# Two transformer blocks on one core: the values' largest magnitude by a matrix product in two steps, and one projection moved ahead of the attention heads

## The chip, the cores and the metric

The kernel runs on one core of a Trainium2 chip. The core has four compute engines with a queue each, which work through their instructions strictly in order: TensorE (PE in the rows; its weight loads stand apart as PEld), VectorE (DVE), ScalarE (ACT) and GpSimd (POOL). SyncE (SP) does nothing here but issue transfers. Engines wait for one another through semaphores. The metric is the device time of one execution in microseconds.

## What is computed

Two blocks follow one another on 512 tokens of width 1024. The first has two kinds of attention and a mixture of experts; the second has a recurrence over time and a latent attention (called MLA below). Cut to what matters here:

```python
def first_block(x, ...):
    h = rms_norm(x, norm_mix_g)
    (f_q, f_k, f_v, f_f, n_q, k_c, v_c, k_s, v_s, k_w, v_w, n_g, g_a, g_b) = split_cols(h @ w_in)
    out_a = from_heads(fox_attention(qa, ka, va, log_f)) @ w_fox_up        # 8 heads of 64, causal
    out_b = from_heads(nsa_attention(qb, kc, vc, ks_, vs_, kw_, vw_, gates)) @ w_nsa_up
    x = x + (sigmoid(g_a) * out_a + sigmoid(g_b) * out_b) @ w_out
    return x + hierarchical_moe(rms_norm(x, norm_ffn_g), ...)              # 16 experts

def second_block(x, ...):
    y_a = rwkv7_branch(...)                                                # recurrence
    y_b = mla_branch(c_q, c_kv, k_pe, z_b, ...)                            # 8 heads of 64, causal
    return x + rmsnorm((g_a * y_a + g_b * y_b) @ w_o, g_post)

# in each attention:  p = softmax(q k^T ...);  out = p @ v
```

## The kernel before, in words

**Two halves.** Products are made nearly exact by splitting an operand x into a coarse part and the rest, x = xh + xl. A projection takes three products per 128 rows of weights (`mm3`: lines 118 to 120), and attention weights and values are split into two 16-bit halves. Sixteen bits have a narrow range, so `Attention.values` first scales a value tensor by 1024 over its largest magnitude. It is called four times: for the 512 value columns of the fox heads (`zv`), for two value groups of 128 columns of the NSA heads (a slice of `kv` and one of `kw`), and for the 512 columns of MLA (`v`).

**The largest magnitude.** VectorE reduces the tensor to one number per partition (`vmx`, line 395). The 128 numbers are written to device memory (line 398) and read back with each partition receiving all of them (`vrow`, line 400). VectorE reduces that row (`vma`, line 402), makes the factor `vsc` and its inverse (lines 403 to 408), ScalarE writes the coarse half (line 414) and VectorE the rest (line 415).

**Heads and fill.** `Attention.run` walks over heads; a head has three units (query tiles 0 and 1, tile 2, tile 3). In turn u it issues the scores of unit u, one preparation step of the next head, the transposes of unit u-1 and the products with the values of unit u-2. The softmax between them is done on VectorE (`s`, `m`) and ScalarE (`p`). Between these pieces `Fill.pull(rate)` issues steps of a list of other work, mostly projections: a projection of 256 columns has 32 products of three matmuls, booked at 0.32 each (3 n / 2400), and a pull of `rate` issues steps until the booked sum is reached. A step without a product has a booking too: each of the six steps that start the NSA heads (`N.start`: gates, norms, values) is booked at 1.0 and puts nothing on TensorE but VectorE and GpSimd work.

**Order.** TensorE's order is exactly that in which the code issues. The other engines' order is set by the scheduler of the build, which the code only suggests. In the first block the fill list is: projections q, k, v of the fox heads, then `kw`, `nq`, the NSA start, gates and output projections. `fill.until("v")` drains it up to the fox values before the heads begin; the rate is 2.0 up to unit 22 and 1.62 after. In MLA the rate is 1.06, and what is left of its list is pulled by the recurrence's preparation.

**Banks.** Accumulators are tiles in eight banks of PSUM. The tag `mm` (projections) has two banks, taken in turn; `x` (preparation of queries and keys) has one. A bank is free again when an engine has read its tile out.

## Time and profile before

| | us |
|---|---|
| median of 3 runs | 1434.35 |
| lowest, highest | 1432.84, 1443.26 |
| the profiled execution | 1437.92 |
| its span, first to last instruction | 1436.0 |
| TensorE busy | 1285.7 (90%) |
| VectorE busy | 951.4 (66%) |
| ScalarE busy | 753.9 (53%) |

The profiled execution is 3.57 us above the median. Busy shares are means over stages with different limits. The fox heads stand at 145 to 300 us of the span, the NSA heads up to 456, the experts at 500 to 880, MLA at 915 to 1045, the recurrence after that. In rows with a time at the front, the first number is the start in us and the second the duration in us; brackets give the idle time of the engine just before and what ended it.

### The profile page before, as it was taken

The numbers are of one execution on the slowest core, as the hardware profiler recorded it, in microseconds if no ns is written. First come the engines' busy times: TensorE is split into PE (matmuls) and PEld (weight loads), VectorE is DVE, ScalarE is ACT, GpSimd is POOL, SyncE is SP. The second block draws the span as 40 slices with busy tenths as digits, with TensorE's granted clock in tenths as the row PEclk, the third lists the DMA queues.
The fourth block names the chain that finished last, engine by engine and source line by source line (L and its number), as shares of the span: only waits on it lengthen the run. The fifth ranks groups of instructions, "written<-read, shape, count | busy, mean of one in ns | idle before, by whom it ended". The sixth has DMA issues, their size and how long they took to land.

```text
span 1436.0 us, 24621 instructions
## 1 busy us (share of the span) xinstructions
PE 1285.7 (90%) x9232; PEld 1090.5 (76%) x9232; DVE 951.4 (66%) x1907; ACT 753.9 (53%) x1291; POOL 427.3 (30%) x349
## 2 busy tenths in 40 slices
PE   7989777997989896899999997879988998799997
PEld 6889677987889775577777776868976767788875
DVE  5565557556565637799999997646657858525645
ACT  5544445665444322688888874645556664224431
POOL 1333324332332111235555522201123335213211
PEclk9999888999999998899999998989999999799999
DMA  6432222222133388999999986521152234233543
GB/s 195 119 106 76 63 54 61 86 64 66 60 96 115 98 285 328 320 356 364 355 345 359 343 292 209 148 83 48 46 165 74 83 123 123 87 100 115 169 135 118
DMA packets 162445, 230.94 MB, mean 161 GB/s; under 512 B 22426, under 2 KB 99021, under 8 KB 162320
## 3 DMA queue, kind: packets, MB, share of 16 engines
q1 hardware_dynamic: 150912, 205.44, 43.7%
q0 software_dynamic: 6224, 18.62, 4.6%
q10 hardware_dynamic: 5184, 5.25, 1.1%
q8 instruction: 74, 1.21, 0.3%
q14 instruction: 51, 0.42, 0.1%
HBM read 200.89 MB, written 30.36 MB: 161 GB/s over the span
## 4 chain that ended last, share of the span: by engine, by line
PE 37%; DVE 9%; DMA 5%; issue 5%; ACT 4%; POOL 1%; POOLq 0%; DVEq 0%; ACTq 0%; SPq 0%
PE mm L118 8%; PE mm L120 8%; PE mm L119 8%; DMA x2d<-y,slt 2%; PE s L120 2%; PE s L118 2%; PE s L119 2%; DMA raw<-in_w_in 2%; PE s L457 1%; DVE itmp L1766 1%; DVE Ti L1768 1%; DMA raw<-in_w_o 1%; PE pt L484 1%; DMA vmmx<-vmx 1%; POOL wl L112 1%
## 5 line engine op out<-in xcount | busy, mean ns | idle before, releaser
L112 POOL TENSOR_TENSOR wl<-raw,wh 128x512 fp32r<-128x512 f32 x119 | 163.7, 1381 | 462.9 <-ACT wh L109 424.2
L92 DVE TENSOR_TENSOR wl<-rawe,wh 128x1024 fp32r<-128x1024 f32 x192 | 224.8, 1218 | 23.9 <-ACT wh L90 22.9
L109 ACT ACTIVATE wh<-raw 128x512 fp32r<-128x512 f32 x214 | 131.6, 627 | 130.2 <-PE mm L120 57.6
L118 PE MATMUL mm<-wh,hh 128*128 128x256 f32 (+1 forms) x616 | 186.7, 303 | 11.1 <-ACT hh L90 3.5
L90 ACT ACTIVATE wh<-rawe 128x1024 fp32r<-128x1024 f32 x192 | 190.6, 1052 | 2.0 <-PE mm L120 1.8
L119 PE MATMUL mm<-wl,hh 128*128 128x256 f32 (+1 forms) x616 | 179.7, 292 | 0.3 <-DVE wl L112 0.3
L120 PE MATMUL mm<-wh,hl 128*128 128x256 f32 (+1 forms) x616 | 179.8, 292 | 0.1
L118 PEld LDWEIGHTS mm<-wh,hh 128*128 128x128 f32 (+1 forms) x616 | 122.8, 199 | 14.3 <-ACT hh L90 3.9
L1262 POOL DMA_INDIRECT xe<-td,slf x16 | 97.9, 6118 | 116.8 <-issue 73.4
L119 PEld LDWEIGHTS mm<-wl,hh 128*128 128x128 f32 (+1 forms) x616 | 122.6, 199 | 2.0 <-DVE wl L112 0.5
L120 PEld LDWEIGHTS mm<-wh,hl 128*128 128x128 f32 (+1 forms) x616 | 122.0, 198 | 0.9 <-DVE hl L92 0.4
L118 PE MATMUL mm<-wh,uh 128*128 128x256 f32 (+1 forms) x352 | 110.4, 314 | 12.9 <-DVE sg L2202 9.3
L112 DVE TENSOR_TENSOR wl<-raw,wh 128x512 fp32r<-128x512 f32 x95 | 79.4, 840 | 58.8 <-ACT wh L109 58.4
L475 ACT ACTIVATE p<-s,m 128x128 f32<-128x128 f32 (+3 forms) x128 | 67.3, 525 | 83.3 <-DVE m L471 62.6
L118 PE MATMUL mm<-wh,xh 128*96 128x512 f32 x256 | 103.8, 405 | 1.3 <-ACT xh L90 1.3
L119 PE MATMUL mm<-wl,uh 128*128 128x256 f32 (+1 forms) x352 | 104.7, 298 | 0.0
L120 PE MATMUL mm<-wh,ul 128*128 128x256 f32 (+1 forms) x352 | 104.5, 297 | 0.0
L120 PE MATMUL mm<-wh,xl 128*96 128x512 f32 x256 | 102.0, 398 | 0.4 <-DVE xl L92 0.4
L119 PE MATMUL mm<-wl,xh 128*96 128x512 f32 x256 | 101.2, 395 | 0.0
L488 DVE SCALAR_TENSOR_TENSOR pl<-pt,ph 128x384 f16<-128x384 f32 (+1 forms) x96 | 57.6, 600 | 39.1 <-ACT ph L487 38.5
L118 PEld LDWEIGHTS mm<-wh,uh 128*128 128x128 f32 x352 | 70.6, 200 | 15.6 <-DVE sg L2202 9.5
L119 PEld LDWEIGHTS mm<-wl,uh 128*128 128x128 f32 x352 | 70.7, 201 | 0.8
(717 smaller groups left out, 3390.0 us busy)
## 6 DMA issues: line engine op xcount, KB each, us to landing
raw<-in_w_in SPq DMA_DIRECT2D x71, 512.0 KB, 3.9
rawe<-in_w_gate SPq DMA_DIRECT2D x64, 512.0 KB, 10.7
rawe<-in_w_down SPq DMA_DIRECT2D x63, 512.0 KB, 11.5
rawe<-in_w_up SPq DMA_DIRECT2D x62, 512.0 KB, 12.1
gd<-sg SPq DMA_DIRECT2D x32, 128.0 KB, 1.9
g<-gd SPq DMA_DIRECT2D x16, 256.0 KB, 3.9
md<-sg ACTq DMA_DIRECT2D x32, 128.0 KB, 2.0
mix<-md SPq DMA_DIRECT2D x16, 256.0 KB, 3.8
```

What stands on the lines that cost most here:

```text
L90: nc.scalar.activation(hi, src, AF.Copy, scale=scale)
L92: nc.vector.tensor_sub(lo, src, hi.bitcast(FT))
L109: nc.scalar.activation(wh, raw[:, k:k + m], AF.Copy)
L112: e.tensor_sub(wl, raw[:, k:k + m], wh.bitcast(FT))
L118: nc.tensor.matmul(out, xh, wh, start=start, stop=False)
L119: nc.tensor.matmul(out, xh, wl, start=False, stop=False)
L120: nc.tensor.matmul(out, xl, wh, start=False, stop=stop)
L457: mm = nc.tensor.matmul(si, q[:, 128 * i:w], k[:, :w], start=a == 0, stop=a == len(passes) - 1)
L475: nc.scalar.activation(p[:, o:o + w], si, AF.Exp, bias=m, scale=-1.0)
L484: nc.tensor.transpose(pt[:, j:j + 128], p[:, j:j + 128], c.ident)
L488: nc.vector.scalar_tensor_tensor(pl[:, :w], pt[:, :w], PSC, ph[:, :w], op0=OP.mult, op1=OP.subtract)
L1262: nc.gpsimd.indirect_dma_start(out=xe, out_offset=None, in_=td, in_offset=bass.IndirectOffsetOnAxis(ap=of, axis=0))
```

## The change

`Attention.values` now returns two functions. The first does the reduction to one number per partition. The second multiplies on TensorE: the 128 numbers, repeated along 128 columns, as one operand and the identity matrix as the other, so that every partition of the result holds all 128 numbers; VectorE reduces that from PSUM. The write to memory and the read back are gone. The product takes a tile of the tag `mm`.

- Fox values: the first function runs where the whole did; the second is step 16 of the 32 products of `kw`.
- `kw` (32 products) moves ahead of the heads: `fill.until("kw")`.
- NSA: the start has eight steps in place of six, still booked at 1.0 each.
- MLA: 3.5 of fill are pulled between the two functions.
- The rate of the first block is 1.64 throughout.

```diff
--- before.py
+++ after.py
@@ -390,30 +390,34 @@
     def values(self, z, nh, pool, name):
 
 
+
         c, nc = self.c, self.c.nc
         mx = c.sm.tile([128, 1], FT, name="vmx")
-        nc.vector.tensor_reduce(mx, z, axis=AX.XY, op=OP.max, apply_absolute_value=True)
-
-        mxd = c.dram.tile([128, 1], FT, name=name + "mx")
-        nc.sync.dma_start(mxd, mx)
-        row = c.sm.tile([128, 128], FT, name="vrow", bufs=1)
-        nc.sync.dma_start(row, _ap(mxd, 0, [[0, 128], [1, 128]]))
-        ma = c.sm.tile([128, 1], FT, name="vma")
-        nc.vector.tensor_reduce(ma, row, axis=AX.X, op=OP.max)
-        nc.vector.tensor_scalar(ma, ma, 1e-30, None, op0=OP.max)
-        sc = c.sm.tile([128, 1], FT, name="vsc")
-        nc.vector.reciprocal(sc, ma)
-        nc.vector.tensor_scalar(sc, sc, PSC, None, op0=OP.mult)
-        back = c.sm.tile([128, 1], FT, name=name + "b", bufs=1)
-        nc.vector.tensor_scalar(back, ma, 1.0 / PSC, None, op0=OP.mult)
-        vh = pool.tile([128, NT, nh, 65], F16, name=name + "h", bufs=1)
-        vl = pool.tile([128, NT, nh, 65], F16, name=name + "l", bufs=1)
-        nc.gpsimd.memset(vh[:, :, :, 64:], 1.0)
-        nc.gpsimd.memset(vl[:, :, :, 64:], 0.0)
-        z = z.rearrange("p i (h d) -> p i h d", d=64)
-        nc.scalar.activation(vh[:, :, :, :64], z, AF.Copy, scale=sc)
-        nc.vector.scalar_tensor_tensor(vl[:, :, :, :64], z, sc, vh[:, :, :, :64], op0=OP.mult, op1=OP.subtract)
-        return vh, vl, back
+
+        def first():
+            nc.vector.tensor_reduce(mx, z, axis=AX.XY, op=OP.max, apply_absolute_value=True)
+
+        def second():
+
+            ps = c.bank("mm", [128, 512])[:, :128]
+            nc.tensor.matmul(ps, mx.to_broadcast([128, 128]), c.ident, start=True, stop=True)
+            ma = c.sm.tile([128, 1], FT, name="vma")
+            nc.vector.tensor_reduce(ma, ps, axis=AX.X, op=OP.max)
+            nc.vector.tensor_scalar(ma, ma, 1e-30, None, op0=OP.max)
+            sc = c.sm.tile([128, 1], FT, name="vsc")
+            nc.vector.reciprocal(sc, ma)
+            nc.vector.tensor_scalar(sc, sc, PSC, None, op0=OP.mult)
+            back = c.sm.tile([128, 1], FT, name=name + "b", bufs=1)
+            nc.vector.tensor_scalar(back, ma, 1.0 / PSC, None, op0=OP.mult)
+            vh = pool.tile([128, NT, nh, 65], F16, name=name + "h", bufs=1)
+            vl = pool.tile([128, NT, nh, 65], F16, name=name + "l", bufs=1)
+            nc.gpsimd.memset(vh[:, :, :, 64:], 1.0)
+            nc.gpsimd.memset(vl[:, :, :, 64:], 0.0)
+            zh = z.rearrange("p i (h d) -> p i h d", d=64)
+            nc.scalar.activation(vh[:, :, :, :64], zh, AF.Copy, scale=sc)
+            nc.vector.scalar_tensor_tensor(vl[:, :, :, :64], zh, sc, vh[:, :, :, :64], op0=OP.mult, op1=OP.subtract)
+            return vh, vl, back
+        return first, second
 
     def run(self, jobs, fill, rate, hooks=()):
 
@@ -647,8 +651,12 @@
 
     qs, two, fx = [], {}, {}
 
+    def largest():
+        fx["first"], fx["second"] = A.values(z["zv"], 8, at, "vf")
+        fx["first"]()
+
     def values():
-        fx["v"] = A.values(z["zv"], 8, at, "vf")
+        fx["v"] = fx["second"]()
 
     def norm(name):
         fx[name] = _head_norm(c, z["z" + name], 512, name, at)
@@ -710,8 +718,9 @@
     jobs = {}
     for name, c0 in (("q", 0), ("k", 512), ("v", 1024)):
         jobs |= {f"{name}{a}": proj("z" + name, {"q": "t0", "k": "zk", "v": "t1"}[name], c0, a) for a in (0, 256)}
-        jobs[name] = ([], [(0.5, values if name == "v" else lambda name=name: norm(name))])
+        jobs[name] = ([], [(0.5, largest if name == "v" else lambda name=name: norm(name))])
     jobs["kw"] = proj("kw", None, 2568, 0, 256)
+    jobs["kw"][1].insert(16, (0.3, values))
     jobs |= {f"nq{a}": proj("nq", "t1", 1544, a) for a in (0, 256)}
     jobs["start"] = ([], [(1.0, f) for f in N.start(A, z, gt)])
     late = []
@@ -766,9 +775,9 @@
     with tc.manual_schedule(engines={mybir.EngineType.PE}):
         N.keys(I, A, z["kv"], fill)
         N.values(I, A, z["kv"], fill)
-        fill.until("v")
+        fill.until("kw")
         comp = [f for g in range(2) for f in N.compressed(g)]
-        A.run([fox(h) for h in range(8)] + N.jobs(A, lambda: big("ob", "zk")), fill, lambda u: 2.0 if u <= 22 else 1.62,
+        A.run([fox(h) for h in range(8)] + N.jobs(A, lambda: big("ob", "zk")), fill, lambda u: 1.64,
               [(43 + 2 * n, f) for n, f in enumerate(comp)])
         fill.until(None)
 
@@ -922,13 +931,17 @@
         def norm(name, z, c0, w):
             self.r[name] = _head_norm(c, proj[z][:, :, c0:c0 + w], w, name, at)
 
-        def values(b, z, c0):
-            v = A.values(proj[z][:, :, c0:c0 + 128], 2, at, "vsw"[b::2])
+        def largest(b, z, c0):
+            self.v[b] = A.values(proj[z][:, :, c0:c0 + 128], 2, at, "vsw"[b::2])
+            self.v[b][0]()
+
+        def values(b):
+            v = self.v[b][1]()
             g = self.gt[:, :, :, b + 1]
             nc.vector.tensor_scalar(g, g, v[2], None, op0=OP.mult)
             self.v[b] = v[:2]
-        return [gates, lambda: norm("n", "nq", 0, 512), lambda: norm("s", "kv", 256, 128), lambda: values(0, "kv", 384),
-                lambda: norm("w", "kw", 0, 128), lambda: values(1, "kw", 128)]
+        return [gates, lambda: largest(0, "kv", 384), lambda: norm("n", "nq", 0, 512), lambda: largest(1, "kw", 128),
+                lambda: values(0), lambda: norm("s", "kv", 256, 128), lambda: values(1), lambda: norm("w", "kw", 0, 128)]
 
     def jobs(self, A, out):
 
@@ -2046,7 +2059,10 @@
         c.mm3(ps, ckv[:, 0, ts], ckv[:, 1, ts], wkh[:, 1].rearrange("p h n -> p (h n)"),
               wkl[:, 1].rearrange("p h n -> p (h n)"), True, True)
         nc.scalar.activation(v[:, i], ps, AF.Copy)
-    vh, vl, vb = A.values(v, 8, ml, "vm")
+    largest, values = A.values(v, 8, ml, "vm")
+    largest()
+    fill.pull(3.5)
+    vh, vl, vb = values()
 
     o = ml.tile([128, NT, 512], FT, name="o", tag="e8", bufs=3)
     z = ml.tile([128, NT, 512], FT, name="z", tag="e8", bufs=3)
```

Rows of the build's order follow. A name is the tile written, then the tiles read.

**VectorE, before the first fox head, before.** `q` and `kl` belong to the queries and keys of head 0; `vfb` and `vwb` are the inverse factors of the fox and of the second NSA values.

```order
L395 TENSOR_REDUCE vmx<-kv 128x1
L112 TENSOR_TENSOR wl<-raw,wh 128x512
L362 SCALAR_TENSOR_TENSOR q<-x,cvec,q 64x512 x2
L402 TENSOR_REDUCE vma<-vrow 128x1
L403 TENSOR_SCALAR vma<-vma 128x1
L405 RECIPROCAL vsc<-vma 128x1
L408 TENSOR_SCALAR vfb<-vma 128x1
L406 TENSOR_SCALAR vsc<-vsc 128x1
L94 SCALAR_TENSOR_TENSOR kl<-x,cvec,kh 128x512
L402 TENSOR_REDUCE vma<-vrow 128x1
L403 TENSOR_SCALAR vma<-vma 128x1
L405 RECIPROCAL vsc<-vma 128x1
```

The same place now:

```order
L405 TENSOR_REDUCE vma<-mm 128x1
L406 TENSOR_SCALAR vma<-vma 128x1
L408 RECIPROCAL vsc<-vma 128x1
L411 TENSOR_SCALAR vfb<-vma 128x1
L409 TENSOR_SCALAR vsc<-vsc 128x1
L418 SCALAR_TENSOR_TENSOR vfl<-zv,vsc,vfh 128x32x64
L112 TENSOR_TENSOR wl<-raw,wh 128x512
L398 TENSOR_REDUCE vmx<-kw 128x1
L112 TENSOR_TENSOR wl<-raw,wh 128x512
L362 SCALAR_TENSOR_TENSOR q<-x,cvec,q 64x512 x2
L94 SCALAR_TENSOR_TENSOR kl<-x,cvec,kh 128x512
```

The reduction `vma` stood between the queries and the keys of head 0; now the whole of the fox values stands ahead of both, and no NSA `vma` is near.

**VectorE at the start of the MLA heads, before.** Tile numbers are kept: `mm` tiles belong to the fill, `x` tiles to queries and keys, `sg` reads a finished fill tile out.

```order
L395 TENSOR_REDUCE vmx_12296<-v_12144 128x1
L165 SCALAR_TENSOR_TENSOR sg_12321<-sg_12321,mm_12269 128x256
L2073 TENSOR_TENSOR qf_12345<-x_12338,csq_11874 128x512
L112 TENSOR_TENSOR wl_12766<-raw_12763,wh_12765 128x512
L92 TENSOR_TENSOR ql_12386<-qf_12345,qh_12385 128x512
L2160 SCALAR_TENSOR_TENSOR sg_12359<-mm_12325,rx_y_11833,br_12267 128x256
L92 TENSOR_TENSOR kl_11971<-x_12377,kh_11970 64x512
L402 TENSOR_REDUCE vma_12302<-vrow_12300 128x1
L92 TENSOR_TENSOR kl_11973<-x_12377,kh_11972 64x512
L403 TENSOR_SCALAR vma_12302<-vma_12302 128x1
L405 RECIPROCAL vsc_12305<-vma_12302 128x1
L408 TENSOR_SCALAR vmb_12308<-vma_12302 128x1
```

The same place now:

```order
L398 TENSOR_REDUCE vmx_12290<-v_12138 128x1
L165 SCALAR_TENSOR_TENSOR sg_12295<-sg_12295,mm_12263 128x256
L112 TENSOR_TENSOR wl_12649<-raw_12646,wh_12648 128x512
L2176 SCALAR_TENSOR_TENSOR sg_12324<-mm_12299,rx_y_11827,br_12261 128x256
L405 TENSOR_REDUCE vma_12347<-mm_12345 128x1
L406 TENSOR_SCALAR vma_12347<-vma_12347 128x1
L408 RECIPROCAL vsc_12350<-vma_12347 128x1
L411 TENSOR_SCALAR vmb_12353<-vma_12347 128x1
L409 TENSOR_SCALAR vsc_12350<-vsc_12350 128x1
L418 SCALAR_TENSOR_TENSOR vml_12356<-v_12138,vsc_12350,vmh_12355 128x32x64
L2089 TENSOR_TENSOR qf_12385<-x_12378,csq_11868 128x512
L2176 SCALAR_TENSOR_TENSOR sg_12390<-mm_12338,rx_y_11827,br_12261 128x256
```

`vma` no longer stands behind `qf`, `ql` and the first `kl` but ahead of them, and `vml`, the long last step of the values, now stands ahead of the queries' `qf` and of the `sg` that reads `mm_12338` out.

**TensorE at the same place, before.** The `x` tile is the keys' product of head 0.

```order
L118 MATMUL mm_12325<-wh_12229,uh_11583 128x256
L119 MATMUL mm_12325<-wl_12230,uh_11583 128x256
L120 MATMUL mm_12325<-wh_12229,ul_11584 128x256
L118 MATMUL mm_12373<-wh_12181,uh_11583 128x256
L119 MATMUL mm_12373<-wl_12182,uh_11583 128x256
L120 MATMUL mm_12373<-wh_12181,ul_11584 128x256
L118 MATMUL x_12377<-ckv_11987,wkh_12138 128x512
L119 MATMUL x_12377<-ckv_11987,wkh_12138 128x512
L120 MATMUL x_12377<-ckv_11987,wkl_12139 128x512
```

And now, from the queries' product on:

```order
L118 MATMUL x_12378<-cq_11980,wqh_12124 128x512
L119 MATMUL x_12378<-cq_11980,wqh_12124 128x512
L120 MATMUL x_12378<-cq_11980,wql_12125 128x512
L118 MATMUL mm_12338<-wh_12223,uh_11577 128x256
L119 MATMUL mm_12338<-wl_12224,uh_11577 128x256
L120 MATMUL mm_12338<-wh_12223,ul_11578 128x256
L118 MATMUL mm_12404<-wh_12175,uh_11577 128x256
L119 MATMUL mm_12404<-wl_12176,uh_11577 128x256
L120 MATMUL mm_12404<-wh_12175,ul_11578 128x256
```

The fill tiles change here. Before, the next tile `mm_12373` follows `mm_12325` in the turn of the two banks. Now the values' product `mm_12345`, issued in the middle of `mm_12338`, has taken a turn, so that `mm_12404` gets the bank of `mm_12338` itself.

## Rows read from the trace of the kernel before

**Rows 1.** The page, part 1: span, and TensorE's line.

```profile
span 1436.0 us, 24621 instructions
PE 1285.7 (90%) x9232; PEld 1090.5 (76%) x9232; DVE 951.4 (66%) x1907; ACT 753.9 (53%) x1291; POOL 427.3 (30%) x349
```

**Rows 2.** Chain that ended last, 940 to 975 us: start, duration, what.

```profile
947.75 9.12 DMA vmmx<-vmx
956.88 3.87 DMA vrow<-vmmx
...
962.32 2.01 ACT vmh L414
964.35 2.35 DVE vml L415
```

**Rows 3.** Tile vrow, its reader's idle times: releaser, us, times.

```profile
  DMA vrow<-smx: 10.2, 1
  DMA vrow<-vmmx: 9.0, 1
  DMA vrow<-vfmx: 7.7, 1
  DMA vrow<-vwmx: 1.5, 1
```

**Rows 4.** Timeline of TensorE: waits.

```profile
162.98 0.47 PE L457 MATMUL s<-kl,q 128*128 128x128 f32 x1 [4.93 <-DVE kl L94]
...
186.08 0.47 PE L457 MATMUL s<-kl,q 128*128 128x128 f32 x1 [9.41 <-DVE kl L94]
...
251.15 0.63 PE L349 MATMUL x<-ident,two 128*128 128x128 f32 x4 [2.39 <-DVE q L362]
...
304.90 0.39 PE L118 MATMUL mm<-wh,hh 128*128 128x256 f32 x1 [1.17 <-ACT sg L155]
...
961.93 0.77 PE L118 MATMUL x<-cq,wqh 128*128 128x512 f32 x1 [6.40 <-DVE vma L403]
```

**Rows 5.** Busy time by stretch; PEclk is TensorE's granted clock.

```profile
core 0: us, PE busy (x) PEld busy (x) DVE busy (x) ACT busy (x) POOL busy (x), PEclk, DMA share, GB/s
...
163.00:168.00 5.00, 5.00 (x23) 4.89 (x23) 3.49 (x8) 3.44 (x7) 2.80 (x1) 0.50 0.04 11
...
186.10:191.80 5.70, 5.70 (x26) 5.61 (x27) 2.80 (x12) 2.53 (x5) 0.00 (x0) 0.50 0.00 0
...
221.30:234.80 13.50, 8.77 (x57) 7.40 (x57) 11.71 (x54) 5.58 (x10) 6.44 (x27) 0.55 0.22 60
...
237.00:300.00 63.00, 59.44 (x601) 56.86 (x601) 39.07 (x110) 39.77 (x77) 24.40 (x23) 1.00 0.25 75
320.00:340.00 20.00, 14.02 (x135) 11.93 (x131) 13.73 (x44) 12.30 (x24) 5.37 (x6) 1.00 0.26 74
...
961.90:973.40 11.50, 9.17 (x29) 6.91 (x29) 6.66 (x12) 6.37 (x9) 0.00 (x0) 0.50 0.24 89
```

**Rows 6.** Timeline of VectorE in MLA.

```profile
960.77 0.29 DVE L402 TENSOR_REDUCE vma<-vrow 128x1 f32<-128x128 f32 x1 [9.01 <-DMA vrow<-vmmx]
...
962.47 0.48 DVE L2160 SCALAR_TENSOR_TENSOR sg<-mm,rx_y,br 128x256 f32<-128x256 f32 x1
...
967.42 0.68 DVE L2073 TENSOR_TENSOR qf<-x,csq 128x512 f32<-128x512 f32 x1
```

**Rows 7.** Timeline of TensorE in MLA: fill and queries.

```profile
946.40 0.39 PE L118 MATMUL x<-cq,wqh 128*128 128x512 f32 x1
...
947.77 0.28 PE L118 MATMUL mm<-wh,uh 128*128 128x256 f32 x1
...
953.29 0.28 PE L118 MATMUL mm<-wh,uh 128*128 128x256 f32 x1
...
953.64 0.28 PE L118 MATMUL mm<-wh,uh 128*128 128x256 f32 x1
```

**Rows 8.** Groups by line: 128x128 32-bit products with the identity.

```profile
L349 PE MATMUL x<-ident,two 128*128 128x128 f32 x80 | 12.7, 283 | 8.4 <-DVE q L362 8.2 <-DVE pc L92 0.3
```

## The prediction

> **What bounds the kernel now.** I read the page first: TensorE is busy 90% of a span of 1436.0 us [rows 1], so time is won only where TensorE waits or runs slowly, and work that is merely moved among its steps is worth nothing. Then the tile that the change deletes. VectorE waits for the read back of the 128 numbers at all four calls, 10.2, 9.0, 7.7 and 1.5 us [rows 3], and the chain that ended last goes through the MLA call: 9.12 us for the write of 128 numbers and 3.87 for the read back [rows 2]. VectorE's queue is in order, so whatever stands behind `vma` waits with it. The timeline of TensorE shows whom that reaches: a wait of 4.93 us and one of 9.41 for the keys `kl` of fox heads, which stand behind the `vma` of the fox values and of the second NSA values, and one of 6.40 in MLA, for the `x` bank that a `kl` behind `vma` reads out [rows 4]. So three of the four round trips reach TensorE.
>
> Each wait is followed by a stretch at 1.2 GHz. The granted clock is 0.50 from 163.0 to 168.0, from 186.1 to 191.8 and from 961.9 to 973.4, with TensorE busy 5.00, 5.70 and 9.17 us in them [rows 5]. At 2.4 GHz that work takes half as long, so the waits cost another 2.5, 2.85 and 4.6 us.
>
> The Trainium skill (DMA: Bandwidth & Descriptors, section Anatomy of one DMA) puts the fixed part of a transfer at about 2.0 us, nearly all of it the confirmation of the write. By that page a pair would take 4.0 us as an estimate, not the 13.0 of rows 2; every wait of TensorE would be nearly covered already, and the change would have only its costs, below. The trace disagrees and decides.
>
> **Removed.** Waits 4.93 + 9.41 + 6.40 = 20.7, slow clock 2.5 + 2.85 + 4.6 = 10.0, together 30.7 us. The 2.3 us that TensorE also idles between 961.9 and 973.4 (9.17 busy of 11.50 [rows 5]) I leave: a softmax chain starts there in either kernel. With the eight small transfers the queue of SyncE no longer holds weight loads behind a read back; I give that nothing, since the loads it delays feed fill that TensorE reaches later.
>
> **Added: the products.** Four products with the identity at some 0.28 us [rows 8]. Those of the two NSA calls fall where TensorE waits anyway. The fox one stands after 16 of the 32 products of `kw`, about 16 x 0.35 = 5.6 us after the reduction was issued (a fill product takes 0.35: the successive starts at 953.29 and 953.64 [rows 7]), so it finds its operand. But it takes a turn of the two `mm` banks, and the third tile of `kw` must then wait until the second, just finished, is read out. The nearest row of such a wait is 1.17 us [rows 4]. Between 0.3 and 1.5 in all; I take 1.0, near that row.
>
> **Moved: `kw` ahead of the heads.** Its 32 products are 11.2 us of full TensorE work that the pulls of 2.0 in units 0 to 22 held before. The lower rate takes 23 x 0.36 = 8.3 booked, 9.1 us in real time, out of those units, and after unit 22 nothing changes to speak of (1.62 to 1.64). If TensorE is the bound in them, they shorten by the 9.1 and the move is free; if the chain of softmax, transposes and bank `x` is the bound, they don't shorten and 9.1 us of waiting appear. From 237 to 300 TensorE was busy 59.44 of 63.00 us at full clock [rows 5], so it is nearly always the bound at the old rate; the idle that is there is mostly for the queries' bank, as the 2.39 us at 251.15 [rows 4]. A tenth thinner cover will widen such waits a little: 2.0, between 0 and 9.1.
>
> **Moved: the start of the NSA heads.** Its steps are booked at 1.0 and put no fill on TensorE. Six at a rate of 2.0 were three units without fill, 221.3 to 234.8: 13.5 us, TensorE busy 8.77 at a mean clock of 0.55, VectorE busy 11.71 [rows 5]. Idle is 4.7; a clock of 0.55 means 12.1 of the 13.5 us at half speed, in which at least 7.4 were busy, which lost 3.7. So 8.4 us were lost, 2.8 per unit, with VectorE the bound. Now eight steps at 1.64 make five units without fill. At 2.8 each they lose 14.0, which is 5.6 more. Against this, VectorE's work there grows only by the later part of two values, and it now has five units to spread over; if the clock held in the whole stretch, 3.7 would come back. Between -3.7 and 5.6, and I take 2.0.
>
> **MLA: a wait that takes the place of the one removed.** The pull of 3.5 (11 products, 3.9 us) covers the reduction, so the product itself waits for nothing. But now `vml` stands on VectorE ahead of the queries' `qf` and of the `sg` that empties `mm_12338`, and the fill tile `mm_12404` needs that very bank. VectorE from `vma` to the end of that `sg`: `vma` and the small ones 0.9 (960.77 to 962.32 less a `kl` of about the size of `qf`), `vmh` on ScalarE 2.0, `vml` 2.35, `qf` 0.68, `sg` 0.48 [rows 2, 6], in all 6.4. TensorE has in that time six fill products, 2.1 us, and the queries, 1.37 (946.40 to 947.77 [rows 7]). It then stands for 6.4 - 3.5 = 2.9 us. The trace of before has no such wait; its nearest kin are the 1.17 above and the 6.40 it replaces [rows 4]. Whether the clock falls after it is open: it held after the 2.39 and fell after the 4.93 [rows 4, 5]; a fall like the first would cost 2.5, like the last 4.6, and I put 1.7. With the product 0.3: 4.9 us, between 1.5 and 11.3.
>
> The 3.5 pulled there are missing in the recurrence's preparation, which pulled what was left of this list. Where TensorE is late there nothing is lost; where it waits for something else, the 3.9 us are added. I take 2.0, the middle.
>
> **The sum.** 30.7 - 1.0 - 2.0 - 2.0 - 4.9 - 2.0 = 18.8 us. The profiled execution took 1437.92 us, its span 1436.0; it becomes 1419.1. It stands 3.57 above the median of the runs, so the median goes from 1434.35 to about **1416**. About 1% (14 us) is what a measurement of this kernel can tell from no change.
>
> **The rivals.** *The heads' units do not shrink.* Their length is set by the chain through VectorE and ScalarE and not by fill; then `kw` is an addition, at 9.1, and the five units lose as the three did, at 5.6. For it speaks that VectorE is nearly full in the stretch without fill, against it 59.44 of 63.00 busy just behind. 30.7 - 1.0 - 9.1 - 5.6 - 4.9 - 2.0 = 8.1, which gives 1426.
>
> *Everything is covered.* The clock holds in the units without fill (-3.7), the MLA wait is only the 1.17 of a plain bank wait with its 0.3, the rest costs 0.3: 30.7 + 3.7 - 1.8 = 32.6, or 1402. For it: VectorE loses its long waits and gets nothing but four short reductions.
>
> *The clock stays down in the heads.* Thinner fill and two more `mm` turns make many short gaps on TensorE, and it is granted 1.2 GHz through units it now runs at full clock. Each busy microsecond at half clock loses half of itself, so the gain is gone when TensorE spends 38 us busy at half clock that it does not now, and the kernel is 1% slower from 66 on. If all of 237 to 300 fell to it, its 59.44 busy us would become 119, and the time 1416 + 59 = 1475. Against it stands 320 to 340: busy only 14.02 of 20.00 in many short gaps, and a clock of 1.00 [rows 5]. The Trainium skill (TensorE: Matmul & The Clock Gate, section A second HAM failure mode: psum-queue depth-cycling) describes just this, short idle times between groups of matmuls that go through the banks in turn, and a clock that goes up and down with them. By that rule this rival would be the likely one; in rows 5 the trace doesn't bear it out at this density of gaps.
>
> *It does not do what it says.* The product comes so late in TensorE's order that VectorE waits for it as it did for the transfer, and the same `kl` waits behind: no gain, 1434. Against it: every reduction is issued microseconds ahead of its product, and no transfer is in between.
>
> **How the numbers follow.** I give the forecast 0.48, units that do not shrink 0.27, everything covered 0.16, the clock 0.04 and no effect 0.05. The forecast's terms spread over some 1407 to 1425. To hold 8 in 10 the range takes in the second case and the nearer part of the third: 1403 to 1430. Faster by over 1% is below 1420: most of the forecast (0.40), all of the third case (0.16) and a little of the second (0.04), 0.60. Slower by over 1% is the clock, 0.04. The rest, 0.36, is within.
>
> **What would show it.** The idle before the first fox scores and before the second head's (4.93 and 9.41) gone, and the clock 1.00 behind both; no `vrow`. In MLA a wait of some 3 us on a fill tile for the `sg` behind `vml`. Five units without fill, and how long they are and at what clock, decides between the forecast and its first two rivals: some 18 to 24 us. The length of fox heads behind them shows whether they shrank: 59.44 of 63.00 would fall to 54 or less if not. Wrong would be the forecast if the clock is low anywhere that it was not, or if the preparation behind MLA grows by more than the 3.9.

## The result and the profile after

The changed kernel took 1419.19 us (median of 4 runs, 1415.48 to 1421.63) beside 1434.04 of the kernel before: ratio 0.9881, 95% interval 0.9847 to 0.9915. A second series gave 1416.74 beside 1435.83, ratio 0.9882, interval 0.9861 to 0.9903. That is 14.9 and 19.1 us less. The forecast was 1416, 3.2 below the first and 0.7 below the second median. The runs differ in TensorE's mean granted clock: in the second series the fastest, 1413.90, had 0.962, the slowest, 1420.44, had 0.953.

The page of the changed kernel, part 1 (compare [rows 1]): TensorE's work is the same, the span is shorter.

```profile
span 1418.3 us, 24618 instructions
PE 1286.9 (91%) x9240; PEld 1090.0 (77%) x9240; DVE 951.1 (67%) x1907; ACT 753.9 (53%) x1291; POOL 426.4 (30%) x349
```

Timeline of TensorE in the changed kernel: the first product and the fill behind it, the first scores with `kl` of fox heads 0 and 1, the first turn of `zq`, the MLA product, two fill products and the keys of MLA, and one wait of the recurrence. Dots stand for rows left out.

```profile
150.66 0.38 PE L403 MATMUL mm<-ident,vmx 128*128 128x128 f32 x2
...
151.39 0.39 PE L118 MATMUL mm<-wh,hh 128*128 128x256 f32 x1 [0.34 <-ACT kw L558]
...
168.82 0.31 PE L461 MATMUL s<-kl,q 128*128 128x128 f32 x1
...
178.78 0.33 PE L461 MATMUL s<-kl,q 128*128 128x128 f32 x1 [0.39 <-DVE kl L94]
...
309.84 0.66 PE L175 MATMUL mm<-ident,zq 128*128 128x128 f32 x4 [2.31 <-ACT sg L1979]
...
936.02 0.49 PE L403 MATMUL mm<-ident,vmx 128*128 128x128 f32 x2 [0.96 <-DVE sg L2176]
...
939.51 0.28 PE L118 MATMUL mm<-wh,uh 128*128 128x256 f32 x1
...
939.87 0.28 PE L118 MATMUL mm<-wh,uh 128*128 128x256 f32 x1
...
942.55 0.50 PE L118 MATMUL x<-ckv,wkh 128*128 128x512 f32 x1 [1.08 <-DVE qf L2089]
...
1076.54 2.08 PE L1703 MATMUL s<-f_r,ones 128*128 128x512 f32 x2 [6.71 <-DVE f_r L1695]
```

The 4.93, 9.41 and 6.40 of [rows 4] have become 0, 0.39 and, in MLA, 0.96 plus 1.08. The product in `kw` costs 0.34 of waiting and 0.38 of its own. Busy time by stretch, columns as in [rows 5]:

```profile
168.00:200.00 32.00, 28.56 (x275) 26.35 (x273) 18.88 (x46) 18.31 (x37) 13.91 (x14) 1.00 0.27 76
200.20:218.30 18.10, 13.62 (x124) 11.87 (x125) 16.90 (x79) 9.68 (x19) 6.03 (x26) 0.91 0.12 39
218.30:285.00 66.70, 61.71 (x618) 58.21 (x617) 44.44 (x128) 40.44 (x80) 25.11 (x24) 1.00 0.26 72
305.00:310.00 5.00, 2.12 (x16) 1.63 (x15) 2.64 (x8) 2.65 (x6) 2.45 (x3) 1.00 0.79 211
310.00:322.00 12.00, 9.90 (x65) 8.48 (x64) 7.76 (x26) 6.23 (x12) 1.04 (x1) 0.57 0.10 35
931.00:950.00 19.00, 16.86 (x121) 15.26 (x120) 11.76 (x20) 9.75 (x16) 2.37 (x2) 1.00 0.47 141
1070.00:1080.00 10.00, 3.46 (x11) 2.01 (x11) 9.97 (x13) 2.92 (x6) 4.55 (x3) 0.59 0.48 134
```

The fox heads run at a clock of 1.00, but for the five units without fill, which take 18.10 us at 0.91. MLA keeps 1.00, where the kernel before had 0.50 [rows 5]. Two places are slower than before. One is 305 to 322, the trigonometric table and the turn of `zq`, with a clock of 0.57 in its later part (the same steps ran at 1.00 in 320 to 340 [rows 5]). The other is the recurrence's preparation, where TensorE waits 6.71 us for a full VectorE (9.97 of 10) and the clock is 0.59 (0.81 in the other execution). In the kernel before, VectorE was as full there, but the wait was 2.51 us:

```profile
1096.81 2.08 PE L1690 MATMUL s<-f_r,ones 128*128 128x512 f32 x2 [2.51 <-DVE f_r L1682]
```

```profile
1090.00:1100.00 10.00, 7.49 (x28) 5.04 (x28) 9.90 (x13) 3.45 (x6) 3.96 (x3) 0.83 0.38 106
```

**Where the time is gained and given back.** The table tells how much earlier a point comes than in the profiled execution of the kernel before, in us. The first microseconds of the kernel vary by a few between executions, so each is counted from the reduction of the fox values (`vmx<-zv`). The columns: the end of heads 1, 9, 12, 13 and 24 (VectorE's `ri`; 9 to 24 are the NSA heads), the reduction in MLA, the second `f_k` read out in the recurrence, the last transposes of the end. The experiments' names are explained below.

| kernel | 1 | 9 | 12 | 13 | 24 | MLA | f_k | end | median, ratio [interval] |
|---|---|---|---|---|---|---|---|---|---|
| changed | 9.8 | 18.1 | 18.9 | 13.2 | 14.0 | 13.2 | 19.4 | 16.8 | 1419.19, 0.9881 [0.9847, 0.9915] |
| changed, again | 9.6 | 17.8 | 18.9 | 13.1 | 13.5 | 13.3 | 18.9 | 19.8 | 1416.74, 0.9882 [0.9861, 0.9903] |
| order alone | -6.1 | -0.5 | 0.0 | -6.3 | -5.0 | 0.1 | -7.1 | -7.0 | 1443.26, 1.0072 [1.0042, 1.0102] |
| product alone | 16.3 | 14.1 | 13.8 | 11.0 | 9.8 | 13.7 | 21.5 | 19.4 | 1416.04, 0.9878 [0.9843, 0.9913] |
| product alone, again | 16.5 | 14.3 | 13.9 | 11.1 | 10.7 | 14.7 | 20.7 | 20.1 | 1420.92, 0.9902 [0.9875, 0.9929] |
| first block only | 9.8 | 16.0 | 17.1 | 11.0 | 10.7 | 10.5 | 13.1 | 10.3 | 1422.84, 0.9914 [0.9879, 0.9948] |
| MLA only | 2.6 | 3.0 | 3.0 | 3.0 | 3.0 | 6.0 | 12.4 | 12.8 | 1427.18, 0.9949 [0.9925, 0.9973] |
| no pull | 10.0 | 17.4 | 18.2 | 14.0 | 14.6 | 16.6 | 23.6 | 24.1 | 1414.15, 0.9875 [0.9840, 0.9911] |
| rates | 8.4 | 14.6 | 16.6 | 18.1 | 17.3 | 17.9 | 23.5 | 24.2 | 1416.67, 0.9880 [0.9855, 0.9905] |
| turn spread | 9.7 | 18.1 | 19.1 | 15.0 | 16.4 | 17.0 | 22.8 | 19.9 | 1415.06, 0.9861 [0.9836, 0.9887] |
| product, turn spread | 16.5 | 14.4 | 14.0 | 13.4 | 7.3 | 6.7 | 13.6 | 13.4 | 1420.59, 0.9900 [0.9874, 0.9925] |
| no pull, turn spread | 8.2 | 16.5 | 17.2 | 13.3 | 14.8 | 17.6 | 25.0 | 24.7 | 1412.76, 0.9865 [0.9842, 0.9889] |
| kw in the heads | 19.5 | 24.4 | 26.6 | 21.0 | 16.3 | 17.0 | 22.6 | 23.2 | 1417.38, 0.9882 [0.9863, 0.9902] |

How far such a column can be trusted is in the table itself. Two executions of one kernel agree within 0.3 us up to head 13, but "MLA only" leaves the fox heads as they were and still shows 2.6 to 3.0 there. The round trips were shorter in that execution: TensorE waited 3.75 and 7.92 us for `kl` where rows 4 have 4.93 and 9.41, together 2.7 less.

```profile
162.88 0.47 PE L489 MATMUL s<-kl,q 128*128 128x128 f32 x1 [3.75 <-DVE kl L94]
...
184.60 0.47 PE L489 MATMUL s<-kl,q 128*128 128x128 f32 x1 [7.92 <-DVE kl L94]
```

So any row may stand 3 us too high against the one execution of before. The experts, the same code everywhere between columns 24 and MLA, add between -0.8 and 5.1.

### The profile page after: what moved, and what is told of

It reads as the page before. It is cut to its first block, busy times and chain, and to the rows that moved or that the text cites. A ratio compares the mean times of both kernels' runs of the same rounds, so it can differ in the third digit from the quotient of the medians.

```text
span 1418.3 us, 24618 instructions
## 1 busy us (share of the span) xinstructions
PE 1286.9 (91%) x9240; PEld 1090.0 (77%) x9240; DVE 951.1 (67%) x1907; ACT 753.9 (53%) x1291; POOL 426.4 (30%) x349
## 4 chain that ended last, share of the span: by engine, by line
PE 50%; DVE 14%; issue 12%; DMA 11%; ACT 7%; POOL 4%; SPq 0%; POOLq 0%; DVEq 0%; ACTq 0%
PE mm L118 11%; PE mm L120 10%; PE mm L119 10%; DMA raw<-in_w_in 5%; PE s L461 3%; POOL wl L112 2%; DMA x2d<-y,slt 2%; PE s L120 2%; PE s L118 2%; ACT wh L109 2%; PE s L119 2%; PE pt L488 1%; DVE wl L112 1%; DVE itmp L1779 1%; DVE Ti L1781 1%
## 5 line engine op out<-in xcount | busy, mean ns | idle before, releaser
L118 PE MATMUL mm<-wh,uh 128*128 128x256 f32 (+1 forms) x352 | 110.3, 313 | 13.6 <-DVE sg L2218 9.1
L118 PEld LDWEIGHTS mm<-wh,uh 128*128 128x128 f32 x352 | 70.1, 199 | 16.5 <-DVE sg L2218 9.3
## 6 DMA issues: line engine op xcount, KB each, us to landing
rawe<-in_w_gate SPq DMA_DIRECT2D x64, 512.0 KB, 10.7
rawe<-in_w_down SPq DMA_DIRECT2D x63, 512.0 KB, 11.1
```

The lines of the kernel that those rows point to most:

```text
L118: nc.tensor.matmul(out, xh, wh, start=start, stop=False)
```

## The experiments

The theory: VectorE's in-order queue is held behind a transfer there and back, and the product removes this. The first rival: the distance between the two steps, and `kw` ahead, do it.

**1. The order alone.** Two steps, `kw` ahead, rate 1.64, pull of 3.5, but the numbers go through memory. The rows of the two NSA groups lie in buffers of another tag; what that does by itself was not tried.

```diff
+        if name in ("vw", "s"):
+            row = pool.tile([128, NT, 32], FT, name="vrow", tag="al", bufs=2).rearrange("p a b -> p (a b)")
+        else:
+            row = c.sm.tile([128, 128], FT, name="vrow", bufs=1)
...
         def first():
             nc.vector.tensor_reduce(mx, z, axis=AX.XY, op=OP.max, apply_absolute_value=True)
+            mxd = c.dram.tile([128, 1], FT, name=name + "mx")
+            nc.sync.dma_start(mxd, mx)
+            nc.sync.dma_start(row, _ap(mxd, 0, [[0, 128], [1, 128]]))
...
-            ps = c.bank("mm", [128, 512])[:, :128]
-            nc.tensor.matmul(ps, mx.to_broadcast([128, 128]), c.ident, start=True, stop=True)
             ma = c.sm.tile([128, 1], FT, name="vma")
-            nc.vector.tensor_reduce(ma, ps, axis=AX.X, op=OP.max)
+            nc.vector.tensor_reduce(ma, row, axis=AX.X, op=OP.max)
```

> The order of the change alone: two steps apart, kw ahead of the heads, rate 1.64, pull of 3.5 in MLA, but the 128 numbers still go through memory; the write and the read back are issued with the reduction. Theory (VectorE's queue is held behind the round trip): fox has 16 products of kw between the steps, 5.6 us, MLA 3.9 us, against some 13 us that the pair took in MLA of before; so VectorE still waits about 7 us for the fox row and about 9 us for the MLA row, the MLA part brings nothing or less than 2 us, and of the first block only the part of head 1 (9.41 + 2.85) is kept: 1421 to 1428 us, 0.991 to 0.996 of before. Rival (the distance between the steps does it, the product is only a means): as the changed kernel, 1419, 0.988 to 0.990, and no wait of VectorE above 2 us for a row.

It took 1443.26, slower than before. Tile `vrow`, its reader's idle time (compare [rows 3]; `smx` is the second NSA group, `vfmx` fox, `vmmx` MLA):

```profile
  DMA vrow<-vfmx: 9.9, 1
  DMA vrow<-vmmx: 8.8, 1
  DMA vrow<-smx: 8.0, 1
```

The chain in MLA, start, duration, what, and TensorE's waits:

```profile
946.08 8.32 DMA vmmx<-vmx
954.42 5.70 DMA vrow<-vmmx
```

```profile
162.62 0.58 PE L118 MATMUL mm<-wh,hh 128*128 128x256 f32 x1 [6.80 <-ACT kw L563]
...
182.59 0.48 PE L466 MATMUL s<-kl,q 128*128 128x128 f32 x1 [4.16 <-DVE kl L94]
...
960.87 0.58 PE L118 MATMUL mm<-wh,uh 128*128 128x256 f32 x1 [6.37 <-DVE vma L411]
```

The pair takes 14.0 us; 5.6 us of `kw` and 3.9 of pulled fill leave VectorE idle for 9.9 and 8.8. The rival falls: distance of this size is not what removes the wait. The theory's number, 1421 to 1428, was wrong too: I expected the part of head 1 to be kept, and 4.16 us of a wait for `kl` were left, behind the `vma` of the second NSA group, and 6.80 us were new in `kw`, whose read-out on ScalarE stands behind `vfh`, which waits for the factor.

**2. The product alone**, in one piece in the place of the transfers.

```diff
-        mxd = c.dram.tile([128, 1], FT, name=name + "mx")
-        nc.sync.dma_start(mxd, mx)
-        row = c.sm.tile([128, 128], FT, name="vrow", bufs=1)
-        nc.sync.dma_start(row, _ap(mxd, 0, [[0, 128], [1, 128]]))
+        ps = c.bank("mm", [128, 512])[:, :128]
+        nc.tensor.matmul(ps, mx.to_broadcast([128, 128]), c.ident, start=True, stop=True)
         ma = c.sm.tile([128, 1], FT, name="vma")
-        nc.vector.tensor_reduce(ma, row, axis=AX.X, op=OP.max)
+        nc.vector.tensor_reduce(ma, ps, axis=AX.X, op=OP.max)
```

> The product alone, in one piece in the place of the round trip; fill order, rates and the MLA pull as before. Theory: the round trips go from VectorE, but TensorE's queue now waits for each reduction in place (about 1 to 3 us at each of the four calls, with the fox and the MLA one on the path). The waits of 4.93 and 9.41 shrink to 2 or less and the 6.40 turns into a wait for the reduction of about 3: gain 10 to 18 us, 1416 to 1424. Rival (the order of the steps is what brings it): TensorE stands for the reduction, the small steps and the later half, as long as it stood for the transfer, 1430 to 1436.

1416.04, ratio 0.9878: the gain of the whole change. TensorE's timeline, then two stretches of it:

```profile
146.12 0.49 PE L398 MATMUL mm<-ident,vmx 128*128 128x128 f32 x2 [3.24 <-DVE vmx L395]
...
931.09 0.49 PE L398 MATMUL mm<-ident,vmx 128*128 128x128 f32 x2 [3.01 <-DVE vmx L395]
```

```profile
146.00:176.00 30.00, 28.33 (x245) 27.47 (x246) 15.23 (x34) 15.71 (x28) 8.16 (x6) 1.00 0.21 62
931.00:956.00 25.00, 23.81 (x181) 21.62 (x181) 17.02 (x32) 15.07 (x27) 1.28 (x1) 1.00 0.32 100
```

TensorE stands for the reduction only, 3.24 and 3.01 us, at two of the four calls, and the clock is 1.00 behind both. The table closes with this: the two waits for `kl` and their slow clock were 19.7 us, less 3.24 that is 16.5, and head 1 ends 16.3 and 16.5 earlier in the two executions. Next to nothing is left there for another cause, such as a queue of SyncE that is free of the read back. Once more beside the changed kernel:

> The product alone in place (the kernel of the second experiment) once more, beside the changed kernel. Theory (the whole gain is the product's, the order adds nothing): within 3 us of the changed kernel. Rival (the order adds a little that the noise of three rounds hid): 4 us or more slower than it.

> The changed kernel itself, once more, as the neighbour of the other three. All theories: 1416 to 1421, 0.986 to 0.991.

1420.92 beside 1416.74, with overlapping intervals. By the medians the difference is 4.2 us: the theory's bound of 3 is missed by 1.2, and the rival's number, 4, is reached. So the product alone is worth 19.3 us in one series (1435.32 - 1416.04) and 14.9 in the other (1435.83 - 1420.92), where the whole change has 19.1. Whether the rest, 0 to 4 us, is the order's is not settled.

**3 and 4. The two halves.** The changed kernel with MLA as before, and the kernel before with MLA changed.

```diff
-    largest, values = A.values(v, 8, ml, "vm")
-    largest()
-    fill.pull(3.5)
-    vh, vl, vb = values()
+    vh, vl, vb = A.values_m(v, 8, ml, "vm")
```

Here `values_m` is the old function; the other kernel makes the opposite edit of the old code.

> The changed kernel with MLA as it was before (round trip through memory in one piece, no pull of 3.5). Theory (the two parts add, the first block is worth about 14 at the end of the experts, MLA about 4 at the end): 1420 to 1424 us, with the first product of MLA 14 us earlier than before, as in the changed kernel, and the end of MLA 13 to 15 earlier. Rival (the preparation behind MLA is bound by VectorE and weight loads and takes back whatever MLA gains): the end is the same as in the changed kernel, 1417 to 1420.

> The kernel before with the MLA part alone (product, two steps, pull of 3.5). Theory: the end of MLA comes 4 to 9 us earlier (6.40 of wait and 4.6 of slow clock removed, 3.9 of pulled fill added, about 2 of new waits), of which the missing fill of the preparation may give back some: 1428 to 1432 us, 0.995 to 0.998. Rival (MLA brings nothing in the end, the gain is all the first block's): 1434, 0.999 to 1.001, with the gain at the end of MLA gone by the end of the preparation.

1422.84 and 1427.18, that is 12.5 and 8.1 less than 1435.32. The sum of 20.6 is close to what the whole gave in its two series, 14.9 and 19.1, so the parts add as far as the noise tells. The rival of the second kernel falls: its ratio has the interval 0.9925 to 0.9973, and the rival asked for 0.999 or more. The first rival's time isn't excluded by its own run (the interval 0.9879 to 0.9948 touches the ratio of the whole change), but its mechanism is, since MLA alone kept its gain to the end. The first kernel's time came as expected, its path did not: MLA's reduction is 10.5 us earlier and not 14. By the medians MLA gave twice the 4 us that I had expected; the interval reaches from 4 to 11.

**5. Without the pull in MLA.**

```diff
     largest()
-    fill.pull(3.5)
     vh, vl, vb = values()
```

> The changed kernel without the pull of 3.5 between the two functions in MLA. Theory (the distance between the steps is worth nothing beside the wait of some 3.0 us that the product alone showed for the reduction at the same place): the product waits 2.5 to 3.5 us for the reduction, MLA's products come earlier by the 3.9 us of fill less that wait, the recurrence's preparation has its fill back, and the time is that of the changed kernel, 1416 to 1421, ratio 0.986 to 0.990. Rival (the pull is needed: without it the wait is followed by a slow clock and the wait for the queries' read-out grows): 4 to 8 us slower than the changed kernel, 1423 to 1427.

1414.15. The wait for the reduction is 3.01, as in experiment 2. From MLA's reduction to the second `f_k`, the table's two columns give 7.0 us gained without the pull (7.8 and 6.0 in the two of "product alone", 6.9 and 7.4 in experiments 8 and 9), and 6.2, 5.6, 6.4, 5.6, 5.8 and 5.6 in the six with the whole MLA edit. By the means, 7.0 and 5.9, the pull is a net loss of 1.1 us; the rival falls. Its slow clock did come in this execution:

```profile
928.00:932.00 4.00, 3.79 (x19) 3.47 (x20) 2.05 (x9) 2.89 (x3) 0.00 (x0) 0.72 0.56 164
932.00:938.00 6.00, 6.00 (x41) 5.51 (x40) 4.79 (x5) 2.10 (x4) 0.00 (x0) 0.90 0.58 199
```

The traces show where the pull loses. The wait for `f_r` in the preparation is 6.68 to 6.72 us in the six kernels with the pull and 2.51 to 2.54 in the five without (2.51 in the kernel before): the 3.9 us of fill that were taken from there leave TensorE idle behind VectorE. From MLA's reduction to the end of the last head (`ri`) the six gain 4.8 us by their mean and the five 8.0; from there to the second `f_k` the six gain 1.0 more and the five lose 1.0. So 3.2 us are spent in MLA and 2.1 come back.

**6. The rates.**

```diff
-        A.run([fox(h) for h in range(8)] + N.jobs(A, lambda: big("ob", "zk")), fill, lambda u: 1.64,
+        A.run([fox(h) for h in range(8)] + N.jobs(A, lambda: big("ob", "zk")), fill, lambda u: 2.0 if u <= 22 else 1.28 if u <= 45 else 1.64,
```

> The changed kernel with a rate of 2.0 up to unit 22, 1.28 up to unit 45 and 1.64 after, so that the same work is pulled by unit 45. Theory (the fox heads' units are as long as TensorE's work in them): the end of fox head 7 comes some 9 us later than in the changed kernel (23 x 0.36 = 8.3 booked, 9.1 in real time) and the difference is gone by the middle of the NSA heads; the whole is 1417 to 1423. Rival (the units are set by the softmax chain, and the lower rate of the changed kernel only made idle time): head 7 ends within 3 us of the changed kernel's, and the lower rate behind unit 22 makes the whole 4 to 9 us faster, 1410 to 1415.

1416.67. The eighth head (fox head 7 of the text above) ends 4.8 us later than in the changed kernel, neither 9 nor under 3, and the ninth 3.5 later. So about half of the 9.1 us of work put back made the units longer, and the rest went into idle time: neither claim holds, and experiment 10 gives a like split. At head 13 this kernel is 4.9 ahead: its turn of `zq` didn't lose anything (16.6 at head 12, 18.1 at 13), though TensorE waited 2.00 us for the table there too.

**7 to 9. The turn of zq spread over the next gate projection**, on the changed kernel, on the product alone, and on the changed kernel without the pull.

```diff
-    jobs["trig"] = ([], [(0.5, lambda: late[0]())])
-    jobs["turn"] = ([], [(1.0, lambda i=i: turn(i)) for i in range(NT)])
     for c0 in range(0, D, 256):
         jobs |= up(c0)
+    for i in reversed(range(NT)):
+        jobs["a0"][1].insert(8 + 8 * i, (1.0, lambda i=i: turn(i)))
+    jobs["a0"][1].insert(0, (0.5, lambda: late[0]()))
```

> The changed kernel with the five steps that put no fill on TensorE around 305 to 322 (the trigonometric table and the four turns of zq, booked at 0.5 and 1.0 each) spread over the tiles of the next gate projection, bookings kept. Theory (the five microseconds that were given back there are idle time and slow clock of a stretch without fill): the shift against the kernel before stays at 18 to 20 at the 13th and the 15th head in place of 14 to 15, the clock stays at 1.00 there, and the whole is 3 to 5 us faster than the changed kernel, 1414 to 1416. Rival (the softmax chain of the two NSA heads there is itself late, since earlier stretches ran ahead): the shift falls to 14 as before, 1418 to 1420.

> The product alone (in place, fill order, rates and MLA as in the kernel before) with the same spreading of the turn of zq. Theory: the product alone gave 0.988, and the spread stretch adds 3 to 5 us: 1411 to 1414, ratio 0.984 to 0.987, the best of all. Rival (the gain of the product alone is the most that the first block can give, later stretches take the rest back): 1415 to 1418.

> The changed kernel without the pull in MLA and with the turn of zq spread. Theory (both were worth some 2 to 4 us by the shifts of their markers, in different stages): 1410 to 1414 us, 3 to 8 us faster than the changed kernel beside it. Rival (what is gained in one stage is given back in the next, by stretches of slow clock that merely move): 1415 to 1419, within 2 us of the changed kernel.

They took 1415.06, 1420.59 and 1412.76. One stretch in the changed kernel, then in the ninth:

```profile
305.00:325.00 20.00, 14.42 (x105) 12.49 (x104) 12.54 (x41) 10.06 (x19) 5.13 (x6) 0.74 0.25 74
```

```profile
305.00:325.00 20.00, 14.86 (x130) 13.59 (x130) 9.43 (x27) 8.86 (x18) 4.20 (x5) 0.91 0.20 67
```

The clock rises to 0.91, but the gain at head 13 still falls, from 19.1 to 15.0 and from 17.2 to 13.3. So the theory of experiment 7 holds for a part only, though its time lies in the range given. In the eighth the loss moved to heads 13 to 24 (13.4 to 7.3), and it missed by 7 us; why is open. The ninth has the lowest median, 4.0 under the changed kernel of its series; the intervals overlap, so this isn't shown.

**10. kw in the heads again**, with the old rates; the rest of the change stays.

```diff
-        fill.until("kw")
+        fill.until("v")
...
-        A.run([fox(h) for h in range(8)] + N.jobs(A, lambda: big("ob", "zk")), fill, lambda u: 1.64,
+        A.run([fox(h) for h in range(8)] + N.jobs(A, lambda: big("ob", "zk")), fill, lambda u: 2.0 if u <= 22 else 1.62,
```

> The changed kernel with kw back behind the start of the heads, and the rates 2.0 and 1.62 of before; the product, the two steps, the eight NSA steps and the pull in MLA stay. Theory (the gain is the product's; where kw stands moves work and no time): 1415 to 1420, within 3 us of the changed kernel; the fox values are ready before the first product with them needs them, and head 0 ends 8 us or so earlier, head 7 equally early. Rival (kw ahead is needed, since it covers the chain from the reduction to the later half of the values): a wait of 3 us or more in front of the first scores or the first product with the values, and 1422 to 1428.

1417.38, as the theory said, but with a miss inside: head 1 ends 9.7 us earlier than in the changed kernel, and head 9 is not equally early but 6.3 us earlier. Its stretches:

```profile
168.00:200.00 32.00, 30.70 (x305) 28.82 (x303) 19.62 (x47) 19.54 (x39) 12.66 (x11) 1.00 0.23 66
...
218.00:285.00 67.00, 64.93 (x652) 61.38 (x650) 45.22 (x129) 42.59 (x85) 25.27 (x24) 1.00 0.26 79
```

TensorE is idle 1.30 and 2.07 us in them; in the changed kernel 3.44 and 4.99. So the thinner cover costs the changed kernel 5 us by head 9. The lead of this kernel is not kept either: between heads 12 and 24 the lead falls from 26.6 to 16.3, and at the start of MLA all but two of the kernels with the product in the first block stand between 13 and 18, whatever the order of their fill (the others: 10.5 and 6.7).

## Why the prediction came out right

The time was right, and so was its main step, that three of the four round trips reach TensorE through VectorE's queue; experiments 1 and 2 show it by taking each half of the change alone. But the 18.8 us net came from terms that missed on both sides: some 9 us against the forecast (cover, turn of `zq`) and 6 to 9 for it (NSA start, MLA, product). That they nearly cancel is luck.

- **Removed in the first block, 19.7 of waits and clock.** Right: both waits are gone and the clock is 1.00 behind.
- **Product in `kw`, 1.0.** 0.34 of waiting, for the read-out that was named, and 0.38 of its own: 0.7.
- **Thinner cover, 2.0 (0 to 9.1).** Mis-sized: 5.0, by the idle time of experiment 10 against the changed kernel. The rival of units that do not shrink was half true: 61.71 busy of 66.70 us is 58.3 of 63.00, between the 59.44 of before and the 54 that the rival asked for.
- **NSA start, 2.0 lost.** Wrong sign. Five units took 18.10 us with 4.48 idle; at a mean of 0.91 at most 3.3 us were at half speed, which lost 1.6 at most. That is 4.5 to 6.1 lost where three units had lost 8.4: 2.3 to 3.9 gained, at the far end of the term's bounds (3.7 gained). In the other execution of the changed kernel the clock was 0.81 in these units with 3.50 idle, 198.6 to 216.7 us; by the same working 1.5 to 3.2 us were gained there. I had priced each unit without fill alike; with more units for the same VectorE work less was idle and less at half speed in all (before: a clock of 0.55).

```profile
198.60:216.70 18.10, 14.60 (x123) 13.04 (x124) 16.63 (x77) 9.88 (x20) 6.31 (x27) 0.81 0.15 47
```

- **Missing: the turn of `zq`.** The sum has no term for it, and some 5.7 us are lost between heads 12 and 13 in both executions. The trace shows a wait of 2.31 us for the table, whose ScalarE step stood behind a weight load, and then a clock of 0.57, where before it held. In ScalarE's queue the order has turned. The table's step (`sg`, 64x512) stands behind `wh`, which waits for a load; in the kernel before and in the product alone it stands ahead of it, and TensorE waits 0.81. First now, then before:

```profile
308.54 0.63 ACT L109 ACTIVATE wh<-raw 128x512 fp32r<-128x512 f32 x1 [1.43 <-DMA raw<-in_w_in]
309.20 0.59 ACT L1979 ACTIVATE sg<-mm 64x512 f32<-64x512 f32 x1
```

```profile
323.01 0.59 ACT L1966 ACTIVATE sg<-mm 64x512 f32<-64x512 f32 x1
324.07 0.63 ACT L109 ACTIVATE wh<-raw 128x512 fp32r<-128x512 f32 x1 [0.47 <-DMA raw<-in_w_in]
```

  The wait is not the whole of it: the product alone loses 2.8 us between these heads with the short wait (13.8 to 11.0), and experiment 6 none with a wait of 2.00. Experiment 7 gives back a part with the clock; why the clock falls here stays open.
- **MLA, a wait of 2.9 for the bank of `mm_12338`.** This step failed. By the build's order the fill product behind the queries (939.51) is the last of `mm_12338`, and the next tile, `mm_12404`, begins at 939.87 without a wait, while the `sg` that empties `mm_12338` starts at 942.41:

```profile
939.54 2.35 DVE L418 SCALAR_TENSOR_TENSOR vml<-v,vsc,vmh 128x2048 f16<-128x2048 f32 x1 [2.12 <-ACT vmh L417]
941.81 0.68 DVE L2089 TENSOR_TENSOR qf<-x,csq 128x512 f32<-128x512 f32 x1
942.41 0.47 DVE L2176 SCALAR_TENSOR_TENSOR sg<-mm,rx_y,br 128x256 f32<-128x256 f32 x1
```

  So the next tile had the other of the two banks, the product's, which is free once `vma` has read it; here the banks were not handed out in turn, as the section on the change had it. The queue that I had read behind `vml` is there, but it reaches TensorE through `qf`, for 1.08 us, and the product itself waits 0.96 for an older read-out. 2.0 in place of 2.9, and the clock stays at 1.00, where I had put 1.7; with the product's 0.49 that is 2.5 in place of 4.9. The two waits are 0.90 to 1.01 and 1.07 to 1.08 in all six executions with this edit.
- **Fill taken from the preparation, 2.0 (0 to 3.9).** Right in size: by the means of experiment 5 the preparation got 2.1 us shorter for the 3.9 us of fill that left it, so 1.8 were lost. The mechanism was the one named: TensorE waits for VectorE there, 6.71 us in place of 2.51.

The first block was forecast at 14.7 net and stands at 13.2 and 14.0 at heads 13 and 24. MLA with its preparation was forecast at 4.1 and gives 5.6 to 6.2 at the second `f_k`. Behind that the two executions of the changed kernel differ by themselves (-2.6 and +0.9). Of its own signs of being wrong one came: the clock is low where it was not, in the turn of `zq`.

The clock rival is out: with 8.4 us of idle time in short gaps, 168 to 200 and 218.3 to 285 ran at 1.00. The rule of the Trainium skill by which it would have been likely (TensorE: Matmul & The Clock Gate, section A second HAM failure mode: psum-queue depth-cycling: short idle times between groups of matmuls make the clock go up and down) is not borne out in these two stretches. On the transfers, the Trainium skill (DMA: Bandwidth & Descriptors, section Anatomy of one DMA — SWDGE (gpsimd) path) has about 2.0 us fixed for each transfer that GpSimd issues. These are issued by SyncE; with that figure all the same, a pair would take an estimated 4.0 us, and experiment 1 would have had next to no wait. Its 8.32 and 5.70 decide.

## What to carry to other kernels

An exchange between partitions by a transfer there and back holds everything that stands behind its reader in that engine's queue; look for whom that reaches, and replace it with a product even if TensorE has to stand for the reduction: it stood 3 us here, and the pair of transfers took 13 to 14. Distances of 5.6 and 3.9 us between the two steps did not help against that, and another engine's read-out then waited for the result; a distance beyond the round trip was not tried. Work that is pulled ahead out of a later stage is only free if TensorE is the bound there: 3.9 us of fill taken from the recurrence's preparation came back as 2.1. When a stage that is bound by TensorE is reordered, count gains at its end, not at its middle: 14 to 24 us at head 9 became 7 to 17 at head 24.

## What was not expected of the hardware

The clock behind one and the same wait differs between executions. In the second series of the product alone, the MLA wait is again 3.01 us; behind it the first stretch below is at 0.50 and full speed comes back after 942, where the other execution of the same kernel had 1.00 throughout. Behind the 3.01 us of experiment 5 it was 0.72.

```profile
934.00:938.00 4.00, 3.70 (x17) 3.67 (x18) 2.15 (x8) 2.23 (x3) 0.00 (x0) 0.50 0.58 168
938.00:942.00 4.00, 4.00 (x20) 3.48 (x20) 2.95 (x2) 0.98 (x2) 0.00 (x0) 0.68 0.50 184
942.00:948.00 6.00, 6.00 (x49) 5.74 (x48) 3.56 (x7) 4.30 (x8) 0.00 (x0) 1.00 0.21 77
```

A slow stretch counted into a single wait's price, as the prediction did, is therefore no fixed price. Nor is the round trip's: TensorE waited 9.41 and 7.92 us for the same `kl` in two executions of the same first block.
